# Attention projection's gate loads moved behind the next pair's weights, and the sample rows' store split over GpSimd's queue

## Chip, cores and metric

The kernel runs on one core of a Trainium2 chip. The metric is the device time of one execution in microseconds; before the change the median of three runs is 2444.72 us (2442.62 to 2445.89).

## The reference

One inference step of a hybrid decoder layer with width 2048, for a prompt of 512 tokens and 8 sequences with 4 new tokens each (544 tokens in all). An input projection feeds two branches: an mLSTM with a matrix memory, and sliding-window attention. Then the two branches are merged, projected and normalized:

```python
br_m = hn.reshape(B, T, M_WIDTH) * jax.nn.sigmoid(o_m) * jax.nn.silu(z_m)
br_a = h_a * jax.nn.silu(z_a)
y = (jax.nn.sigmoid(g_m) * jnp.einsum('btc,cd->btd', br_m, w_proj_m)
     + jax.nn.sigmoid(g_a) * jnp.einsum('btc,cd->btd', br_a, w_proj_a))
out = jnp.einsum('btc,cd->btd', y, w_out)
return _layernorm(DN_ALPHA * x + out, ln_w, ln_b).astype(x.dtype)
```

The change touches the product with `w_proj_a` and its gate `sigmoid(g_a)`, and the store of the normalized rows of the 32 sample tokens. All is float32.

## The kernel before

Each float32 operand is split into a high part and a low remainder: ScalarE casts the weights (L208, "wh"), VectorE subtracts (L209, "wl"), and TensorE adds three products (L699 with wh, L701 with wl). Activations lie transposed, 128 features by 544 tokens.

**A pair of column tiles.** For most of the projections two neighbouring tiles of 128 output columns are computed together, by a Strassen-like scheme (`paired`, L731): seven half products (steps 0 to 6) of sums of four weight blocks b11, b12, b22, b21 and sums of activation blocks that were stored earlier. `load_a` fetches b11 and b12 (L195, 512 KB each), `load_b` b22 and b21 (L668, 512 KB each). `prepare` makes the weight sums: t1 = b11 + b12 and b11 = t1 + b22 on VectorE (L679), and in a projection that has "acc" set, b12 += b22 and b21 += b11 by accumulating DMAs on GpSimd's queue (L677). `gather` collects the seven results.

**The attention projection.** Its first eight tiles and the last two are single; the six from tile 8 (PAIR_A) to 14 (TAIL_A) are three pairs, made by `pair_a` (L1774). Each pair also needs two gate tiles of 128x544 (272 KB each) from `d_sga`, the sigmoid stored in device memory; L1787 multiplies them with the pair's results, and L1788 stores the products to `d_t`. The gate tiles come from the pool `c5`, which has two buffers, so a gate load waits until the store that last used the buffer has landed. In the loop of `paired`, the call `early()` of a pair (which issues its gate loads, L1782) comes in that pair's step 2, `load_a` of the next pair in step 3 and `load_b` in step 4:

```python
if n == 3:
    load_a(work[p])
elif n == 4:
    load_b(work[p])
```

A scheduler orders the instructions of each engine by these places in the program and by priorities (weights' preparation is raised by AHEAD); SP issues the loads in its own order and, when one has to wait, all behind it wait.

**The end.** The output rows are normalized in row tiles of 128 tokens, 0 to 3 for the prompt; row 4 stands for the 32 sample tokens, held in `zs` as 128 partitions (four groups of 512 columns by 32 tokens). Row tiles 2, 3 and the samples are finished while the products for row tiles 0 and 1 run; those two come last. `moments` takes the mean and variance of a row tile, with the power -1/2 on GpSimd (L1993). `finish(4)` scales `zs`, adds the bias by an accumulating DMA of GpSimd (L2000), and stores it by one DMA of SP (L2001), in which the output is seen as 4x32x512. SP then issues the stores of row tile 0 (L2170) and of row tile 1 (L2011); ScalarE's queue issues one of each (L2170).

Of the kernel before, what the change touches and what calls it, by code (L numbers as in the profile page):

```python
# [18 lines left out]
ALU = mybir.AluOpType  # L19
# [55 lines left out]
def _build(tc, nc, i, o, es):  # L75
# [12 lines left out]
    V, A, G, PE = nc.vector, nc.scalar, nc.gpsimd, nc.tensor  # L88
# [43 lines left out]
    state = {}  # L132
# [27 lines left out]
    mh = cst.tile([128, 8], F32, name="mh")  # L160
# [27 lines left out]
    def kview(name):  # L188
        return i[name].rearrange("(kt p) c -> p kt c", p=128)
# [145 lines left out]
    for g in range(8):  # L335
        for q in range(2):
# [13 lines left out]
            else:  # L350
                hilo(pt[:], xk2[0][k // 4 - 2][:, k % 4, 0:SEQ], xk2[1][k // 4 - 2][:, k % 4, 0:SEQ])
                x_cast = state["x_cast"]
                c = (slice(None), k - 8, slice(0, SEQ - HT))
                state["x_end"] = V.tensor_tensor(out=s1r[c], in0=pt[:, HT:SEQ], in1=s1r[c], op=ALU.subtract)
        if g % 2:
# [8 lines left out]
            else:  # L364
                hilo(src, *(xk2[p][g // 2 - 2][:, :, SEQ:T] for p in range(2)))
                c = (slice(None), slice(k4.start - 8, k4.stop - 8), slice(SEQ - HT, HT))
# [295 lines left out]
    def load_a(w):  # L662
        w["b11"], w["b12"] = (load_half(w["wv"], c0, 0) for c0 in (w["cA"], w["cB"]))

    def load_b(w):
        for n, c0 in (("b22", w["cB"]), ("b21", w["cA"])):
            w[n] = raw2()
            state["load"] = nc.sync.dma_start(w[n][:], w["wv"][:, 8:16, c0:c0 + 128])  # L668

    def prepare(w, n):  # L670


        def add(out, a, b):
            if w.get("acc") and out == a and n != 2:
                loaded = state.get(("sums", 13))
                with tc.issue_after(loaded.ins) if loaded else ExitStack():
                    G.dma_start(out=w[out][:], in_=w[b][:], accum_op=ALU.add)  # L677
            else:
                V.tensor_tensor(out=w[out][:], in0=w[a][:], in1=w[b][:], op=ALU.add)  # L679
        if n == 1:  # L680
            w["t1"] = raw2()
            add("t1", "b11", "b12")
        elif n == 2:
            add("b11", "t1", "b22")
        w["hl", n] = split(w[("b11", "t1", "b11", "b21", "b12", "b22", "b21")[n]])
        if n == (1 if w.get("acc") else 3):
            add("b12", "b12", "b22")
        elif n == (3 if w.get("acc") else 4):
            add("b21", "b21", "b11")
# [42 lines left out]
    def paired(work, plain=None, rest=()):  # L732

        steps = [(w, n) for w in work for n in range(7)]
        ready = 0
        with tc.issue_after(state["load"].ins):
            load_a(work[0])
            load_b(work[0])
        for at, (w, n) in enumerate(steps):

            while ready < min(at + 3, len(steps)):
                with tc.high_priority(offset=AHEAD), tc.issue_after(plain.ins) if plain else ExitStack():
                    prepare(*steps[ready])
                ready += 1
            p = at // 7 + 1
            if p < len(work):
                if n == 3:
                    load_a(work[p])
                elif n == 4:
                    load_b(work[p])  # L750
            if n == 2 and "early" in w:
                w["early"]()
            if at == 4:
                for _ in rest:
                    pass
            half_product(w, n)
            with tc.high_priority(offset=AHEAD):
                gather(w, n)
            if n == 6:
                w["end"](w["O1"], w["O2"])  # L760
            tick()
# [907 lines left out]
    wm, wa_, wo = kview("w_proj_m"), kview("w_proj_a"), kview("w_out")  # L1669
# [104 lines left out]
    def pair_a(ct):  # L1774

        sgs = []

        def early():
            for c in (ct, ct + 1):
                sg = c5t()  # L1780
                with tc.issue_after(state["load"].ins):
                    nc.sync.dma_start(sg[:], d_sga[c])  # L1782
                sgs.append(sg)

        def end(o1, o2):
            for c, sg, o in zip((ct, ct + 1), sgs, (o1, o2)):
                V.tensor_tensor(out=sg[:], in0=o[:], in1=sg[:], op=ALU.mult)  # L1787
                nc.sync.dma_start(d_t[c], sg[:])  # L1788
        return dict(wv=wa_, x=XA, cA=ct * 128, cB=ct * 128 + 128, scale=1.0, acc=True, end=end, early=early)

    LEAD_A, PAIR_A, TAIL_A = 6, 8, 14
    marks = []
# [37 lines left out]
    XA = operands((bah_, bal_), SA)  # L1830
# [93 lines left out]
    zs = d0.tile([128, 512], F32, name="zs")[:]  # L1924
    stt = d0.tile([128, 5, 4, 6], F32, name="stt")
    mv = d0.tile([128, 5, 4], F32, name="mv")
    ys_rows = y_s.rearrange("b t d -> (b t) d")
# [51 lines left out]
    def moments(t):  # L1979
        m = mv[:, t]  # L1980
        if t < 4:
            V.bn_aggr(m[:, 0:2], stt[:, t])
            V.tensor_scalar(m[:, 1:2], m[:, 1:2], EPS, None, op0=ALU.add)
        else:
            V.bn_stats(stt[:, t, 0], zs)
            V.bn_aggr(m[:, 0:2], stt[:, t, 0:1])
            V.scalar_tensor_tensor(m[:, 1:2], m[:, 0:1], m[:, 0:1], m[:, 1:2], op0=ALU.mult, op1=ALU.add)
            pm = sm()
            PE.matmul(pm[:, 0:2], cq, m[:, 0:2], start=True, stop=True)
            V.tensor_copy(m[:, 0:2], pm[:, 0:2])  # L1990
            V.scalar_tensor_tensor(m[:, 3:4], m[:, 0:1], m[:, 0:1], m[:, 1:2], op0=ALU.mult, op1=ALU.subtract)
            V.tensor_scalar(m[:, 1:2], m[:, 3:4], -1.0, EPS, op0=ALU.mult, op1=ALU.add)
        G.tensor_tensor(out=m[:, 2:3], in0=m[:, 1:2], in1=mh[:, 0:1], op=ALU.pow)  # L1993

    def finish(t, cuts=(0, 512, 1280, D), plain=0):

        if t == 4:
            V.scalar_tensor_tensor(zs, zs, mv[:, t, 0:1], lwq, op0=ALU.subtract, op1=ALU.mult)
            A.activation(zs, zs, AF.Copy, scale=mv[:, t, 2:3])
            G.dma_start(out=zs, in_=lbq, accum_op=ALU.add)  # L2000
            nc.sync.dma_start(ys_rows.rearrange("r (q c) -> q r c", q=4), zs)  # L2001
            return
        parts = [(c0, c1, weighed(t, c0, c1)) for c0, c1 in zip(cuts, cuts[1:])]
        added(t, parts[plain:])
        for part in parts[:plain]:
            shifted(t, *part)
# [6 lines left out]
    def weighed(t, c0, c1):  # L2013
        zt = zcol(c0, c1 - c0)[:, t]
        V.scalar_tensor_tensor(zt, zt, mv[:, t, 0:1], state["ln_w"][:, c0:c1], op0=ALU.subtract, op1=ALU.mult)
        return zt
# [12 lines left out]
    def add_rows(t):  # L2029

        zt = zcol(D - G3 * 128, G3 * 128)[:, t]
        V.scalar_tensor_tensor(zt, zt, ALPHA, rows[t][:, 0:G3 * 128], op0=ALU.mult, op1=ALU.add)
        stats(t, t + 1, 3)
        moments(t)
# [76 lines left out]
    for g in range(G3):  # L2111
        ct = 16 - G3 + g
# [30 lines left out]
    for q in range(4):  # L2143
        r, cs = slice(q * 32, q * 32 + 32), slice(q * 512, q * 512 + 512)
# [50 lines left out]
    copied = [scaled(0, q, zt) for q, zt in enumerate(state["w0"])]  # L2195
    with tc.high_priority(offset=4000):
        add_rows(1)
        w1 = [weighed(1, *c) for c in QUARTERS]
        with tc.issue_after(copied[1].ins):
            factors(1)  # L2200
        biases([(1, 0, sm())])
        scaled(1, 0, w1[0])
        for q in (1, 2, 3):
            shifted(1, *QUARTERS[q], w1[q], behind=state["stored"])
# [30 lines left out]
```

## Time and profile before

| | us |
|---|---|
| median of 3 runs | 2444.72 (2442.62 to 2445.89) |
| the profiled execution's own time | 2444.07 |
| its span | 2442.3 |
| TensorE busy | 2425.5 (99%) |
| VectorE busy | 1910.9 (78%) |
| ScalarE busy | 1251.8 (51%) |
| GpSimd busy | 528.7 (22%) |

The span runs from the first to the last instruction of the profiled execution; its own time is 1.8 us longer. Busy time is the time in which an engine computed; issuing a DMA and waiting are not counted. In the rows below, "SPq" is SP's queue of DMA issues, "PE" TensorE, "DVE" VectorE, "ACT" ScalarE, "POOL" GpSimd. A timeline's row has the start, the length, the engine, the line, the operation with out<-in, and in brackets the idle time before it with what ended that. q0 is the queue of the DMAs that GpSimd issues, q1 that of SP.

### The profile page before, as it was taken

How to read it: one execution, taken by the hardware profiler on the slowest of the kernel's cores; microseconds unless marked ns; L12 is line 12 of the kernel's file. 1: busy time of each engine (PE TensorE's matmuls, PEld its weight loads, DVE VectorE, ACT ScalarE, POOL GpSimd, SP SyncE). 2: the span in 40 equal slices, each digit the busy share in tenths (PEclk: the TensorE clock that was granted, in tenths of full speed). 3: DMA queues.
4: the chain of work that ended last, by engine and by line, in shares of the span. 5: the costliest groups of instructions: out<-in, count | busy, mean ns of one | idle time of the engine just before them, and what ended most of it. 6: DMA issues, size and time to landing. Idle time of an engine off the chain costs nothing.

```text
span 2442.3 us, 49020 instructions
## 1 busy us (share of the span) xinstructions
PE 2425.5 (99%) x19394; PEld 2371.8 (97%) x19394; DVE 1910.9 (78%) x2879; ACT 1251.8 (51%) x2074; POOL 528.7 (22%) x505
## 2 busy tenths in 40 slices
PE   9999999999999999999999999999999999999998
PEld 8999999999999999999999999999999999999997
DVE  7868888888888888987877888878865676877656
ACT  6456676676666665433433444444644444444432
POOL 4114333333333430211111221120000120111111
PEclk9999999999999999999999999999999999999999
DMA  6876676667777655677687676687764598898776
GB/s 180 204 173 158 159 166 146 159 155 177 169 171 176 164 146 146 153 228 238 180 252 241 172 237 212 183 248 222 246 203 160 181 257 245 228 237 269 204 220 192
DMA packets 569601, 479.88 MB, mean 196 GB/s; under 512 B 48604, under 2 KB 464076, under 8 KB 569116
## 3 DMA queue, kind: packets, MB, share of 16 engines
q1 hardware_dynamic: 550908, 411.48, 57.1%
q0 software_dynamic: 17984, 64.50, 13.4%
q8 instruction: 152, 2.49, 0.4%
q10 hardware_dynamic: 480, 0.79, 0.1%
q14 instruction: 77, 0.63, 0.1%
HBM read 326.35 MB, written 100.77 MB: 175 GB/s over the span
## 4 chain that ended last, share of the span: by engine, by line
PE 95%; DMA 2%; DVE 1%; issue 1%; ACT 0%; POOL 0%; DVEq 0%; SPq 0%; POOLq 0%; ACTq 0%
PE bank L699 48%; PE bank L701 24%; PE bank L218 9%; PE sm L1528 2%; PE bank L1335 1%; PE sm L1567 1%; PE sm L814 1%; PE sm L1583 1%; PE sm L865 1%; PE sm L218 1%; PE sm L2047 1%; PE sm L840 1%; PE sm L1340 1%; DMA raw<-in_w_out 1%; DMA xr<-in_x_prompt 0%
## 5 line engine op out<-in xcount | busy, mean ns | idle before, releaser
L208 ACT CAST wh<-raw 128x1024 fp32r<-128x1024 f32 x641 | 671.6, 1048 | 823.2 <-PE bank L699 698.6
L209 DVE TENSOR_TENSOR wl<-raw,wh 128x1024 fp32r<-128x1024 f32 x641 | 803.6, 1254 | 194.3 <-ACT wh L208 182.2
L699 PE MATMUL bank<-xk,wh 128*128 128x272 f32 x2336 | 323.4, 289 | 0.0
L679 DVE TENSOR_TENSOR raw<-raw,raw 128x1024 f32<-128x1024 f32 x244 | 309.5, 1269 | 14.3 <-DMA raw<-in_w_proj_a 5.7
L699 PEld LDWEIGHTS bank<-xk,wh 128*128 128x128 f32 x2336 | 303.4, 188 | 1.9 <-issue 1.4
L718 POOL TENSOR_TENSOR ev<-p,ev 128x272 f32<-128x272 f32 x85 | 117.3, 1380 | 450.0 <-ACT ev L717 423.9
L699 PE MATMUL bank<-n2h,wh 128*128 128x272 f32 x656 | 170.0, 291 | 0.0
L701 PE MATMUL bank<-xk,wl 128*128 128x272 f32 x1168 | 169.8, 287 | 0.0
L699 PE MATMUL bank<-n3h,wh 128*128 128x272 f32 x656 | 169.5, 291 | 0.2 <-ACT wh L208 0.2
L699 PE MATMUL bank<-s1h,wh 128*128 128x272 f32 x656 | 169.6, 291 | 0.0
L699 PE MATMUL bank<-n2l,wh 128*128 128x272 f32 x656 | 168.0, 287 | 0.0
L699 PE MATMUL bank<-n3l,wh 128*128 128x272 f32 x656 | 167.7, 288 | 0.0
L699 PE MATMUL bank<-s1l,wh 128*128 128x272 f32 x656 | 167.4, 287 | 0.2 <-DVE s1l L258 0.2
L699 PE MATMUL bank<-s4h,wh 128*128 128x272 f32 x656 | 167.5, 289 | 0.0
L699 PE MATMUL bank<-s4l,wh 128*128 128x272 f32 x656 | 167.0, 287 | 0.0
L701 PEld LDWEIGHTS bank<-xk,wl 128*128 128x128 f32 x1168 | 155.5, 188 | 0.1
L677 POOL DMA_DIRECT2D raw<-raw x96 | 83.2, 866 | 319.4 <-DVE ev L726 220.7
L699 PE MATMUL bank<-a11h,wh 128*128 128x272 f32 x584 | 150.5, 289 | 0.0
L699 PE MATMUL bank<-a11l,wh 128*128 128x272 f32 x584 | 149.4, 288 | 0.0
L699 PEld LDWEIGHTS bank<-n3h,wh 128*128 128x128 f32 x656 | 123.4, 188 | 2.1 <-issue 1.2
L699 PEld LDWEIGHTS bank<-s1h,wh 128*128 128x128 f32 x656 | 123.2, 188 | 1.6 <-issue 1.0
L699 PEld LDWEIGHTS bank<-n2h,wh 128*128 128x128 f32 x656 | 123.4, 188 | 1.2 <-issue 1.2
(551 smaller groups left out, 5792.5 us busy)
## 6 DMA issues: line engine op xcount, KB each, us to landing
raw<-in_w_in SPq DMA_DIRECT2D x296, 512.0 KB
raw<-raw POOLq DMA_DIRECT2D x96, 512.0 KB, 5.0
C<-in_state_mlstm_C SPq DMA_DIRECT2D x32, 1024.0 KB
out<-C SPq DMA_DIRECT2D x64, 512.0 KB
raw<-in_w_proj_a SPq DMA_DIRECT2D x32, 512.0 KB
raw<-in_w_proj_m SPq DMA_DIRECT2D x32, 512.0 KB
raw<-in_w_out SPq DMA_DIRECT2D x32, 512.0 KB
d_v<-ev SPq DMA_DIRECT2D x16, 272.0 KB
```

What stands on the lines that cost most here:

```text
L208: state["cast"] = A.copy(wh[:, k:k + n], raw[:, k:k + n])
L209: state["split"] = V.tensor_tensor(out=wl[:, k:k + n], in0=raw[:, k:k + n], in1=r32(wh[:, k:k + n]), op=ALU.subtract)
L218: PE.matmul(ps[f][:, :w], a[:, kk], b(k, c, w), start=(k == 0 and n == 0), stop=(k == 15 and n == 2))
L677: G.dma_start(out=w[out][:], in_=w[b][:], accum_op=ALU.add)
L679: V.tensor_tensor(out=w[out][:], in0=w[a][:], in1=w[b][:], op=ALU.add)
L699: PE.matmul(ps, wh[:, k], x(p, k), start=(first and k == 0 and p == 0), stop=False, skip_group_check=True)
L701: state["end"] = PE.matmul(ps, wl[:, k], x(0, k), start=False, stop=(k == 7), skip_group_check=True)
L718: G.tensor_tensor(out=c22, in0=p1, in1=c11, op=ALU.subtract)
L814: PE.matmul(pp[:, c0 + w0:c0 + 256], qs[a][:, j * 128:j * 128 + 128], kx[:, k0:k0 + 256 - w0], start=(n == 0), stop=(n == 1))
L840: PE.transpose(pt[:, b * 128:b * 128 + 128], s_[:, b, 128:256], ident)
L865: PE.matmul(po[:, b * 128:b * 128 + n], VA[:, b], p_[:, 2 * b:2 * b + n // 128], start=(b == 0 and m == 0), stop=(b == 3 and m == 1), skip ...
L1528: state["cells"] = PE.matmul(pp[:, 0:258], a[:, b * 128:b * 128 + 128], b_[:, b, f], start=(b == 0 and n == 0), stop=(b == 3 and n == 2))
```

## The change

The two gate loads of each attention pair are issued in step 4, behind both loads of the next pair, and no longer in step 2 (`early_at`). The other users of `paired` keep step 2. The sample rows are stored by four DMAs of 32x512 (64 KB each) that GpSimd issues after its power for row tile 1; SP's transfer is gone. From L1790 on, lines shift by one to three.

```diff
@@ -748,7 +748,7 @@
                     load_a(work[p])
                 elif n == 4:
                     load_b(work[p])
-            if n == 2 and "early" in w:
+            if n == w.get("early_at", 2) and "early" in w:
                 w["early"]()
             if at == 4:
                 for _ in rest:
@@ -1786,7 +1786,8 @@
             for c, sg, o in zip((ct, ct + 1), sgs, (o1, o2)):
                 V.tensor_tensor(out=sg[:], in0=o[:], in1=sg[:], op=ALU.mult)
                 nc.sync.dma_start(d_t[c], sg[:])
-        return dict(wv=wa_, x=XA, cA=ct * 128, cB=ct * 128 + 128, scale=1.0, acc=True, end=end, early=early)
+        return dict(wv=wa_, x=XA, cA=ct * 128, cB=ct * 128 + 128, scale=1.0, acc=True, end=end, early=early,
+                    early_at=4)
 
     LEAD_A, PAIR_A, TAIL_A = 6, 8, 14
     marks = []
@@ -1990,7 +1991,7 @@
             V.tensor_copy(m[:, 0:2], pm[:, 0:2])
             V.scalar_tensor_tensor(m[:, 3:4], m[:, 0:1], m[:, 0:1], m[:, 1:2], op0=ALU.mult, op1=ALU.subtract)
             V.tensor_scalar(m[:, 1:2], m[:, 3:4], -1.0, EPS, op0=ALU.mult, op1=ALU.add)
-        G.tensor_tensor(out=m[:, 2:3], in0=m[:, 1:2], in1=mh[:, 0:1], op=ALU.pow)
+        state["power"] = G.tensor_tensor(out=m[:, 2:3], in0=m[:, 1:2], in1=mh[:, 0:1], op=ALU.pow)
 
     def finish(t, cuts=(0, 512, 1280, D), plain=0):
 
@@ -1998,7 +1999,6 @@
             V.scalar_tensor_tensor(zs, zs, mv[:, t, 0:1], lwq, op0=ALU.subtract, op1=ALU.mult)
             A.activation(zs, zs, AF.Copy, scale=mv[:, t, 2:3])
             G.dma_start(out=zs, in_=lbq, accum_op=ALU.add)
-            nc.sync.dma_start(ys_rows.rearrange("r (q c) -> q r c", q=4), zs)
             return
         parts = [(c0, c1, weighed(t, c0, c1)) for c0, c1 in zip(cuts, cuts[1:])]
         added(t, parts[plain:])
@@ -2195,6 +2195,9 @@
     copied = [scaled(0, q, zt) for q, zt in enumerate(state["w0"])]
     with tc.high_priority(offset=4000):
         add_rows(1)
+        with tc.issue_after(state["power"].ins):
+            for q in range(4):
+                G.dma_start(out=ys_rows[:, q * 512:q * 512 + 512], in_=zs[q * 32:q * 32 + 32])
         w1 = [weighed(1, *c) for c in QUARTERS]
         with tc.issue_after(copied[1].ins):
             factors(1)
```

On SP, between the first and the second pair, before the change (raw_3320 and raw_3321 are b22 and b21 of the first pair, raw_24470 is b12 and raw_3347, raw_3348 are b22 and b21 of the second pair, raw_24701 is b11 of the third; c_3338 and c_3339 are the first pair's gates):

```order
L668 DMA raw_3320_24339<-in_w_proj_a 128x8x128
L668 DMA raw_3321_24341<-in_w_proj_a 128x8x128
L1782 DMA c_3338_24432<-d_sga 128x544
L1463 DMA c_3416_25122<-d_brm 128x544
L1772 DMA d_t<-c_3308_24204 128x544
L668 DMA raw_3347_24503<-in_w_proj_a 128x8x128
L1782 DMA c_3339_24434<-d_sga 128x544
L1463 DMA c_3420_25144<-d_brm 128x544
L195 DMA raw_24470<-in_w_proj_a 128x8x128
L195 DMA raw_24701<-in_w_proj_a 128x8x128
L668 DMA raw_3348_24505<-in_w_proj_a 128x8x128
L1788 DMA d_t<-c_3339_24434 128x544
```

The first pair's gates stand ahead of b12 of the second pair. The same place in the changed kernel (raw_24466 is now b12, raw_24697 b11 of the third pair, raw_3345 and raw_3346 b22 and b21 of the second, c_3347 and c_3348 the gates):

```order
L668 DMA raw_3321_24341<-in_w_proj_a 128x8x128
L1463 DMA c_3416_25122<-d_brm 128x544
L1772 DMA d_t<-c_3308_24204 128x544
L668 DMA raw_3345_24499<-in_w_proj_a 128x8x128
L1463 DMA c_3420_25144<-d_brm 128x544
L195 DMA raw_24466<-in_w_proj_a 128x8x128
L195 DMA raw_24697<-in_w_proj_a 128x8x128
L668 DMA raw_3346_24501<-in_w_proj_a 128x8x128
L1782 DMA c_3347_24503<-d_sga 128x544
L1782 DMA c_3348_24505<-d_sga 128x544
L1788 DMA d_t<-c_3348_24505 128x544
```

Both gates now stand behind b12, b11 and b21. VectorE's order around the end of the first pair is the same before and after; in the changed kernel it reads (raw_3351 is t1, raw_24464 b11 of the second pair):

```order
L209 TENSOR_TENSOR wl_24533<-raw_24464,wh_24532 128x1024
L679 TENSOR_TENSOR raw_3351_24561<-raw_24464,raw_24466 128x1024
L1787 TENSOR_TENSOR c_3348_24505<-ev_24423,c_3348_24505 128x544
L679 TENSOR_TENSOR raw_24464<-raw_3351_24561,raw_3345_24499 128x1024
L728 SCALAR_TENSOR_TENSOR ev_24422<-bank_24432,p_3330_24384 128x272
L209 TENSOR_TENSOR wl_24564<-raw_3351_24561,wh_24563 128x1024
L1787 TENSOR_TENSOR c_3347_24503<-ev_24422,c_3347_24503 128x544
L209 TENSOR_TENSOR wl_24599<-raw_24464,wh_24598 128x1024
```

The multiply with the second gate tile stands between the two weight sums of the second pair. GpSimd's end:

```order
-L2000 DMA zs<-room_29415 128x512
-L1993 TENSOR_TENSOR mv<-mv,mh 128x1
-L2231 UNCONDITIONAL_BRANCH
-L2231 ISA
+L1994 TENSOR_TENSOR mv<-mv,mh 128x1 x2
+L2001 DMA zs<-room_29415 128x512
+L1994 TENSOR_TENSOR mv<-mv,mh 128x1
+L2200 DMA out<-zs 32x512 x4
+L2234 UNCONDITIONAL_BRANCH
+L2234 ISA
```

Four stores follow the last power; on SP the row of L2001 is gone, and nothing else of the end moves.

## Rows read from the trace of the kernel before

**Rows 1.** The page: span and busy time of the engines.

```profile
span 2442.3 us, 49020 instructions
...
PE 2425.5 (99%) x19394; PEld 2371.8 (97%) x19394; DVE 1910.9 (78%) x2879; ACT 1251.8 (51%) x2074; POOL 528.7 (22%) x505
```

**Rows 2.** Waits of TensorE, whole kernel: line, releaser: us, times, longest.

```profile
PE bank L699 <- ACT wh L208: 1.3, 2, 1.1
```

**Rows 3.** Chain, 1975 to 2003 us: start, length, what.

```profile
1984.26 8.28 DMA raw<-in_w_proj_a
...
1992.66 1.24 DVE raw L679
...
1995.09 3.78 PE bank L699 x28
```

**Rows 4.** Waits of SP's queue, 1971 to 1984 us.

```profile
SPq L1782 <- DMA d_t<-c: 9.0, 1, 9.0
```

**Rows 5.** Timeline of SP, 1960 to 2024 us: start, length, what.

```profile
1973.16 0.38 SPq L668 DMA_DIRECT2D raw<-in_w_proj_a  x1
1982.59 0.32 SPq L1782 DMA_DIRECT2D c<-d_sga  x1
...
1986.94 2.33 SPq L668 DMA_DIRECT2D raw<-in_w_proj_a  x1
...
2003.83 3.66 SPq L195 DMA_DIRECT2D raw<-in_w_proj_a  x2
2007.58 1.54 SPq L668 DMA_DIRECT2D raw<-in_w_proj_a  x1
```

**Rows 6.** Timeline of VectorE, 1960 to 2024 us.

```profile
1981.51 1.23 DVE L209 TENSOR_TENSOR wl<-raw,wh 128x1024 fp32r<-128x1024 f32 x1 [1.13 <-ACT wh L208]
...
1993.80 0.72 DVE L1787 TENSOR_TENSOR c<-ev,c 128x544 f32<-128x544 f32 x1
1994.43 1.22 DVE L679 TENSOR_TENSOR raw<-raw,raw 128x1024 f32<-128x1024 f32 x1
...
2014.09 0.72 DVE L1787 TENSOR_TENSOR c<-ev,c 128x544 f32<-128x544 f32 x1
...
2016.21 1.21 DVE L209 TENSOR_TENSOR wl<-raw,wh 128x1024 fp32r<-128x1024 f32 x1
```

**Rows 7.** Timeline of ScalarE, 1960 to 2024 us.

```profile
1995.77 1.05 ACT L208 CAST wh<-raw 128x1024 fp32r<-128x1024 f32 x1 [0.73 <-DVE raw L679]
```

**Rows 8.** Windows: length, busy us by engine, PEclk, DMA share, GB/s.

```profile
1993.00:1994.00 1.00, 1.00 (x9) 0.79 (x7) 1.00 (x2) 0.01 (x1) 0.00 (x0) 1.00 1.17 302
1994.00:1995.00 1.00, 0.01 (x1) 0.00 (x0) 1.00 (x2) 1.00 (x1) 0.81 (x1) 1.00 0.78 195
```

**Rows 9.** DMA queues, 1997 to 1998 us: packets, MB, share.

```profile
q0 software_dynamic: 48, 0.20, 106.5%
```

**Rows 10.** Timeline of TensorE, 2013 to 2020 us.

```profile
2018.25 1.17 PE L701 MATMUL bank<-sumh,wl 128*128 128x272 f32 x8
```

**Rows 11.** Windows of the end, columns as in rows 8.

```profile
2434.00:2439.00 5.00, 0.00 (x0) 0.00 (x0) 0.52 (x1) 0.44 (x1) 0.00 (x0) 1.00 0.99 365
2439.50:2441.00 1.50, 0.00 (x0) 0.00 (x0) 0.00 (x0) 0.00 (x0) 0.00 (x0) 0.50 0.24 90
2441.00:2442.30 1.30, 0.00 (x0) 0.00 (x0) 0.00 (x0) 0.00 (x0) 0.00 (x0) 0.50 0.00 0
```

**Rows 12.** DMA issues, 2424 to 2443 us: KB each, us to landing.

```profile
zs<-room POOLq DMA_DIRECT2D x1, 256.0 KB, 4.8
```

**Rows 13.** Timeline of GpSimd (POOL), 2422 to 2443 us.

```profile
2425.84 0.87 POOL L2000 DMA_DIRECT2D zs<-room  x1 [0.47 <-ACT room L2161]
2429.98 0.99 POOL L1993 TENSOR_TENSOR mv<-mv,mh 128x1 f32<-128x1 f32 x1 [3.28 <-DVE mv L1983]
```

**Rows 14.** Timeline of SP, 2422 to 2443 us.

```profile
2430.70 0.61 SPq L2001 DMA_DIRECT2D out<-zs  x1
...
2434.54 3.13 SPq L2011 DMA_DIRECT2D out<-zr  x3
```

## The prediction

> **What bounds the kernel now.** I read the page first. TensorE is busy for 2425.5 of the 2442.3 us of the span [rows 1], so a change can only give back what lies in TensorE's few gaps, or behind its last product. The waits of TensorE come next. Away from the first microseconds, where it waits for inputs, its largest is on L699, for a cast of weights on ScalarE: 1.3 us in two waits, the longest 1.1 [rows 2]. The chain of waits says which gap that is: between the first two pairs of the attention projection, and what ended last there was a weight load of L195 that was issued at 1984.26 and took 8.28 us; then came the sum t1 of L679, a cast, and L699 at 1995.09 [rows 3]. So at this place DMA is late, by about a microsecond, and nowhere else inside the kernel. The end is the second place: VectorE, ScalarE and TensorE are done by about 2434.5, and the rest is output stores.
>
> Why is that load late? It is b12 of the second pair. Its buffer comes free with the L209 of step 4 of the first pair, 1981.51 + 1.23 = 1982.74 [rows 6]. But SP works its queue in order, and ahead of b12 stands the second gate tile, which waited 9.0 us for a store of d_t [rows 4] and went out at 1982.59, with a d_brm load behind it [rows 5]. So b12 left 1.5 us after it could, and with two tiles of 272 KB ahead of it.
>
> A measurement of this kernel can tell about 0.2%, 4.9 us, from no change.
>
> **The move of the gate loads.** It adds and removes no instruction: three pairs, two loads each, change places on SP. The third pair has no next pair, and its loads keep their place: nothing. For the first pair, b12 is no longer behind the gate tile. The d_brm load now ahead of it waits only for a use of its buffer long past. So b12 leaves at about 1982.8 and lands at least 1.5 us earlier; the sum t1 (1992.66) and the cast follow, and the gap of 1.1 us closes, since it is shorter than that. **Gain 1.1 us** on the path, and TensorE starts step 1 of the second pair at 1995.09 - 1.1 = 1994.0.
>
> What is late next? The gate tiles are now the last in SP's queue, behind b12, b11 of the third pair, and b21. The b21 load went out at 1986.94 + 2.33 = 1989.3 [rows 5], so the gates go out after that. The bytes in the queue are the same as before, and the queue was full: DMA share 1.17 in 1993 to 1994 and 0.78 in the next microsecond, 302 and then 195 GB/s [rows 8]. It ran dry near 1994.8. A tile that is last in a queue lands when the queue runs dry: **not before 1994.8**. The latest: with t1 earlier, GpSimd issues the accumulating copy b12 += b22 earlier, and its bytes go ahead of the gates. It moves 512 KB at 0.20 MB per us, and in 1997 to 1998, while one ran, no other queue moved a packet, though a b22 load had just been issued on SP [rows 9]: 2.6 us. And the first gate tile, loaded some 30 us before its use until now, is 272 KB more at 0.30 MB per us, 0.9 us, if some engine stood idle earlier. So 1994.8 + 2.6 + 0.9 = 1998.3 at the latest.
>
> Who waits? VectorE's order is t1, then the multiply by the second gate (L1787), and only then the sum b11 = t1 + b22 of step 2 (L679), at 1993.80 and 1994.43 [rows 6]; the cast of step 2 began at 1995.77 and took 1.05 [rows 7]. From the landing G of the second gate to the weights of step 2 is thus 0.63 + 1.34 + 1.05 = 3.0 us. TensorE wants them after the 16 matmuls of step 1's first part: 28 of them took 3.78 us [rows 3], so 16 take 2.2, and the need is at 1994.0 + 2.2 = 1996.2. The stall is G + 3.0 - 1996.2, or G - 1993.2: 1.6 to 5.1 us, and at the middle (G = 1996.5) 3.3. Both ends rest on rows that are equally near, so I take the middle. Less the 1.1 gained: **+2.2 us** (0.5 to 4.0).
>
> The same move between the second and third pair. Before, no gap of TensorE stood there. The b21 load left at 2007.58 + 1.54 = 2009.1 [rows 5] and the gates now go behind it. The earliest landing is b21 and two gates, 1.08 MB at 0.30 MB per us, after that: 2012.7. The latest adds 512 KB of weights queued ahead (1.7 us) and the accumulating copy (2.6): 2017.0. From the multiply at 2014.09 to the L209 of step 1 at 2016.21 and its end is 2.12 + 1.21 = 3.3 us [rows 6]; TensorE wants that at 2018.25 [rows 10]. So a landing up to 2014.9 costs nothing, and the latest 2.1 us. All of it moves along with the first stall. I take the middle of the cost: **+1.0 us** (0 to 2.1).
>
> One cast on ScalarE and its subtraction on VectorE swap places with their neighbours before the second pair; each waits for work that was ready, and both engines have idle time there: nothing.
>
> **The sample rows' store.** Before, one SP transfer of 256 KB was issued at 2430.70, taking 0.61 us of SP, ahead of SP's six stores for row tiles 0 and 1; the issues of the last three ended at 2434.54 + 3.13 = 2437.7 [rows 14]. The stretches of the end: 365 GB/s at a share of 0.99 from 2434 to 2439, then 90 GB/s at a share of 0.24, about 4 of 16 engines, from 2439.5 to 2441, then nothing for 1.3 us [rows 11]. The slow stretch fits the store in which the transfer's outermost size is 4. It moves 0.135 MB, which at 365 GB/s takes 0.4 us and not 1.5: 1.1 us. The first stores of row tile 0 leave 0.7 us earlier, into a time in which the DMA engines were not full. **Gain 1.8 us.** The bounds: 0.3 us, if the slow stretch is another store's, and 2.8, if the stores behind it find their engines free a microsecond sooner as well.
>
> GpSimd now issues four transfers behind the power of L1993, which ended at 2430.97. One issue takes 0.87 [rows 13]: done at 2434.5. The accumulation of 256 KB before it took 4.8 us to land [rows 12], so the four land by 2439.3, 1.7 us before the last byte now. Nothing stands behind them on GpSimd. Cost: nothing, and if that cover is gone (a landing of 4.8 us becomes 6.5), each further microsecond is a microsecond.
>
> **The sum** against the profiled execution's own 2444.07 us: 2444.07 + 2.2 + 1.0 - 1.8 = 2445.5. That execution lies 0.65 us under the median of the runs shown, 2444.72, so I forecast 2446.1: no change that can be told.
>
> **The rivals.** *The gates land in time.* SP is no longer held for 9.0 us behind a gate's buffer [rows 4], so loads that stood behind it can move up into earlier time. If the engines had room there, the queue runs dry before 1993.2 and nothing stalls. Then 2444.07 - 1.1 - 1.8 = 2441.2, or 2441.8 as a median: faster than before. It decides at a landing of 1994.3, where stall and gain are equal. Against it: a share over 1 up to 1994 [rows 8].
>
> *Both accumulating copies go wholly ahead of the gates.* +4.0 + 2.1 - 1.8 gives 2449.0 as a median, and with the small gain at the end 2450.5. For it: SP's queue stood still during such a copy [rows 9].
>
> *The end gains only the issue time.* The slow stretch may be a store of row tile 1 whose engines fell behind; then the bytes are the same and only SP's 0.61 us are saved: 2445.5 + 1.2 = 2446.7, as a median 2447.3. The Trainium skill, "DMA: Bandwidth & Descriptors", section "Rules for kernel authors", holds that spreading transfers over the issuing engines gives no bandwidth, since all use the same 16 engines, and saves issue time alone. By that rule this rival is the case; a share of 0.24 [rows 11] speaks against it, since the engines were not all at work.
>
> **How the numbers follow.** Forecast (the gates stall TensorE, the end is shorter) 0.60, with its own range 2443.5 to 2448.5; gates in time 0.20; both copies ahead 0.12; issue time alone 0.08. The range 2441.2 to 2450.2 holds the forecast, the third rival and most of the other two. Faster by over 0.2% would be below 2439.8, which needs more than both gains at once: 0.06. Slower by over 0.2% is above 2449.6: 0.12, the second rival's upper part and stalls that I don't see. Within: 0.82.
>
> **What would show it.** Right: b12's issue at about 1982.8, no wait of L699 in step 1 of the second pair, but a wait of a few microseconds in step 2, for ScalarE's cast, with VectorE's L1787 released by the load of d_sga and the gates landing last; no stretch of about 90 GB/s at the end, and the span's end about 1.8 us sooner after TensorE's last matmul. Wrong: L1787 not released by a DMA; a gap of more than 5 us; GpSimd's four stores landing after all others.

## The result and the profile after

The changed kernel takes 2449.73 us in the median of 22 runs (2446.54 to 2452.64); the kernel before, on the same chip, 2445.56 us (22 runs, 2442.07 to 2449.73). The ratio is 1.0017, with a 95% interval of 1.0010 to 1.0023: 4.2 us slower, between 2.4 and 5.6. That is clear of zero, so it is a loss, though a smaller one than the 0.2% (4.9 us) that I had said a measurement can tell. The forecast was 2446.1 in a range of 2441.2 to 2450.2. The profiled execution took 2449.24 us, with a span of 2447.5, against 2444.07 and 2442.3.

The span is 5.2 us longer in these two executions. Where that comes from is read by placing the same instructions of both side by side. VectorE's L724 of the first attention pair (step 4) and L724 of a pair some 160 us later bracket the moved loads; first the kernel before, then the changed one (timeline of VectorE: start, length, engine, line):

```profile
1986.97 0.44 DVE L724 SCALAR_TENSOR_TENSOR ev<-bank,ev 128x272 f32<-128x272 f32 x1 [1.97 <-PE bank L701]
...
2143.38 0.44 DVE L724 SCALAR_TENSOR_TENSOR ev<-bank,ev 128x272 f32<-128x272 f32 x1 [1.42 <-PE bank L701]
```

```profile
1988.35 0.44 DVE L724 SCALAR_TENSOR_TENSOR ev<-bank,ev 128x272 f32<-128x272 f32 x1 [2.38 <-PE bank L701]
...
2150.62 0.44 DVE L724 SCALAR_TENSOR_TENSOR ev<-bank,ev 128x272 f32<-128x272 f32 x1 [1.42 <-PE bank L701]
```

The bracket is 156.41 us long before and 162.27 after: **5.9 us were lost between these two rows.** The first pair itself starts 1.4 us later in the changed kernel's execution; 1.3 of that is there by 100 us into the span, where nothing was changed. The last row of VectorE (L2009) is the bracket of the end, again before and after:

```profile
2432.45 2.07 DVE L2009 SCALAR_TENSOR_TENSOR zr<-zr,mv,pk 128x512 f32<-128x512 f32 x3
```

```profile
2438.93 2.07 DVE L2009 SCALAR_TENSOR_TENSOR zr<-zr,mv,pk 128x512 f32<-128x512 f32 x3
```

From its start to the end of the span it is 2442.3 - 2432.45 = 9.85 us before, 2447.5 - 2438.93 = 8.57 after: **1.3 us were gained at the end.** Between the bracket and L2009 the changed kernel makes up another 0.8 us (it is 7.24 us behind at the bracket's second row, 6.48 at L2009); what does that is not shown.

What stands inside the longer bracket is told by the waits of TensorE from 1960 to 2060 us, in the changed kernel:

```profile
PE bank L699 <- ACT wh L208: 4.4, 1, 4.4
PE bank L701 <- DVE wl L209: 0.4, 1, 0.4
```

The wait before step 1 of the second pair [rows 2, 3] is gone. A new one of 4.4 us stands in step 2. SP's timeline and VectorE's around it:

```profile
1980.30 0.32 SPq L1463 DMA_DIRECT2D c<-d_brm  x1
1983.72 5.00 SPq L195 DMA_DIRECT2D raw<-in_w_proj_a  x2
1988.82 0.54 SPq L668 DMA_DIRECT2D raw<-in_w_proj_a  x1
1989.41 4.48 SPq L1782 DMA_DIRECT2D c<-d_sga  x2
```

```profile
1992.11 1.22 DVE L679 TENSOR_TENSOR raw<-raw,raw 128x1024 f32<-128x1024 f32 x1
1999.13 0.73 DVE L1787 TENSOR_TENSOR c<-ev,c 128x544 f32<-128x544 f32 x1 [5.80 <-issue]
1999.77 1.22 DVE L679 TENSOR_TENSOR raw<-raw,raw 128x1024 f32<-128x1024 f32 x1
```

The row of L195 holds b12 and b11 of the third pair; b12 is out at 1983.72, right after its buffer is free, and t1 (L679, 1992.11) starts without a wait. The gates are issued last, from 1989.41 on. VectorE then stands idle for 5.80 us in front of the multiply by the second gate (1999.13), with the weight sum of step 2 behind it (1999.77). The profile names no releaser here ("issue"). The trace's record of semaphores does: the semaphore of each load is updated 16 times, and for the second gate tile the last of the 16 came at 1999.05, 0.08 us ahead of the multiply. In runs 4, 1 and 8 below it came at 2000.17, 2001.43 and 1999.60, and the multiply again 0.08 us behind it. The chain of waits goes on through the cast to TensorE, and windows show the granted clock (PEclk, third column from the right):

```profile
2001.10 1.05 ACT wh L208
...
2002.20 3.09 PE bank L699 x12
2005.28 1.81 PE bank L701 x8
...
2007.72 0.99 PE bank L701 x8
```

```profile
1997.00:1999.00 2.00, 0.78 (x7) 0.56 (x5) 0.00 (x0) 0.00 (x0) 0.00 (x0) 1.00 1.15 253
2000.00:2002.00 2.00, 0.00 (x0) 0.00 (x0) 2.00 (x3) 0.90 (x1) 0.00 (x0) 0.61 0.42 147
2002.00:2007.00 5.00, 4.80 (x21) 4.81 (x22) 2.25 (x3) 1.49 (x3) 0.00 (x0) 0.50 0.53 159
2007.00:2008.00 1.00, 1.00 (x9) 1.00 (x8) 0.81 (x1) 0.64 (x2) 0.39 (x1) 0.87 0.02 9
```

From the multiply's start to TensorE's start it is 2002.20 - 1999.13 = 3.07 us, the 3.0 of the forecast. But the 12 matmuls then take 3.09 us and 8 take 1.81, where 8 at the full clock take 0.99 a little later: the granted clock had fallen to 0.50, the lower of TensorE's two levels (1.2 GHz of 2.4), while the engine stood still, and it came back by about 2007. TensorE's busy time is 2427.9 us, 2.4 more than [rows 1]. So the bracket is accounted for by +4.4 (wait), +2.4 (clock), +0.4 (the wait of L701 between the second and third pair), -1.1 (the old wait): 6.1, against 5.9 measured.

The end: GpSimd's four stores are issued behind the power; the stretches of the last 1.5 us before the last byte show no slow one of the kind in [rows 11]:

```profile
2437.47 2.08 POOL L2200 DMA_DIRECT2D out<-zs  x4
```

```profile
2444.50:2445.00 0.50, 0.00 (x0) 0.00 (x0) 0.00 (x0) 0.00 (x0) 0.00 (x0) 0.50 1.05 397
2445.00:2445.50 0.50, 0.00 (x0) 0.00 (x0) 0.00 (x0) 0.00 (x0) 0.00 (x0) 0.50 0.48 180
2445.50:2446.00 0.50, 0.00 (x0) 0.00 (x0) 0.00 (x0) 0.00 (x0) 0.00 (x0) 0.50 0.08 29
```

397 GB/s, then 180, then 29: within a microsecond the rate falls to nearly nothing, and no stretch near 90 GB/s at a share of 0.24 stands there any more.

### The profile page after: what moved, and what is told of

It reads as the page before. It is cut to its first block, busy times and chain, and to the rows that moved or that the text cites. A ratio compares the mean times of both kernels' runs of the same rounds, so it can differ in the third digit from the quotient of the medians.

```text
span 2447.5 us, 49023 instructions
## 1 busy us (share of the span) xinstructions
PE 2427.9 (99%) x19394; PEld 2374.8 (97%) x19394; DVE 1910.0 (78%) x2879; ACT 1252.3 (51%) x2074; POOL 532.5 (22%) x509
## 4 chain that ended last, share of the span: by engine, by line
PE 98%; DVE 1%; issue 0%; ACT 0%; SPq 0%; DMA 0%; DVEq 0%; ACTq 0%
PE bank L699 49%; PE bank L701 24%; PE bank L218 10%; PE sm L1528 2%; PE sm L218 2%; PE bank L1335 1%; PE sm L1567 1%; PE sm L814 1%; PE sm L1583 1%; PE sm L865 1%; PE sm L2047 1%; PE sm L840 1%; PE sm L1340 1%; PE bank L421 0%; PE sm L1515 0%
## 5 line engine op out<-in xcount | busy, mean ns | idle before, releaser
L699 PE MATMUL bank<-xk,wh 128*128 128x272 f32 x2336 | 323.4, 289 | 0.0
L679 DVE TENSOR_TENSOR raw<-raw,raw 128x1024 f32<-128x1024 f32 x244 | 309.7, 1270 | 10.1 <-DMA raw<-in_w_in 2.7
L699 PEld LDWEIGHTS bank<-xk,wh 128*128 128x128 f32 x2336 | 303.4, 188 | 1.9 <-issue 1.4
L699 PE MATMUL bank<-n2h,wh 128*128 128x272 f32 x656 | 170.0, 291 | 0.0
L701 PE MATMUL bank<-xk,wl 128*128 128x272 f32 x1168 | 169.8, 287 | 0.0
L699 PE MATMUL bank<-n3h,wh 128*128 128x272 f32 x656 | 169.5, 291 | 0.2 <-ACT wh L208 0.2
L699 PE MATMUL bank<-s1h,wh 128*128 128x272 f32 x656 | 169.6, 291 | 0.0
L699 PE MATMUL bank<-n2l,wh 128*128 128x272 f32 x656 | 167.9, 287 | 0.0
L699 PE MATMUL bank<-n3l,wh 128*128 128x272 f32 x656 | 167.7, 288 | 0.0
L699 PE MATMUL bank<-s4h,wh 128*128 128x272 f32 x656 | 167.5, 289 | 0.0
L699 PE MATMUL bank<-s1l,wh 128*128 128x272 f32 x656 | 167.3, 287 | 0.0
L699 PE MATMUL bank<-s4l,wh 128*128 128x272 f32 x656 | 167.0, 287 | 0.0
L701 PEld LDWEIGHTS bank<-xk,wl 128*128 128x128 f32 x1168 | 155.6, 188 | 0.1
L677 POOL DMA_DIRECT2D raw<-raw x96 | 83.2, 867 | 314.2 <-DVE ev L726 217.7
L699 PE MATMUL bank<-a11h,wh 128*128 128x272 f32 x584 | 150.5, 289 | 0.0
L699 PE MATMUL bank<-a11l,wh 128*128 128x272 f32 x584 | 149.4, 288 | 0.0
L699 PEld LDWEIGHTS bank<-n3h,wh 128*128 128x128 f32 x656 | 123.4, 188 | 2.1 <-issue 1.2
L699 PEld LDWEIGHTS bank<-s1h,wh 128*128 128x128 f32 x656 | 123.2, 188 | 1.6 <-issue 1.0
L699 PEld LDWEIGHTS bank<-n2h,wh 128*128 128x128 f32 x656 | 123.4, 188 | 1.2 <-issue 1.2
```

Of the source, the lines that this page charges most:

```text
L699: PE.matmul(ps, wh[:, k], x(p, k), start=(first and k == 0 and p == 0), stop=False, skip_group_check=True)
L701: state["end"] = PE.matmul(ps, wl[:, k], x(0, k), start=False, stop=(k == 7), skip_group_check=True)
```

## Experiments

My theory after the result, **A**: the gates land last, VectorE's multiply waits and holds up the weight sum behind it, TensorE waits and then runs at half the clock; the end gains 1.3 us. Its rivals are named with the runs. Each run below is one kernel; ratios are against the kernel before on the same chip.

**1. Only the gate loads moved.**

```diff
-            if n == 2 and "early" in w:
+            if n == w.get("early_at", 2) and "early" in w:
...
+                    early_at=4)
```

> Only the move of the gate loads; the sample rows are stored by SP's one transfer as before. Theory A (the gates land last, VectorE's multiply holds up the weight sum of step 2 of the second pair, TensorE waits and its clock falls): the wait of L699 for the cast stays near 4.4 us, TensorE is at a granted clock of 0.50 for some 5 us after it, and without the end's gain of 1.3 us the time is 5 to 6 us over the kernel before (ratio 1.002 to 1.0025). Rival B (the loss comes from the stores of GpSimd at the end): the time is that of the kernel before, within 1 us.

2452.17 us, ratio 1.0029 (1.0019 to 1.0038), 7.1 us slower. The waits of TensorE from 1960 to 2060 us:

```profile
PE bank L699 <- ACT wh L208: 7.1, 1, 7.1
```

So the loss is the gates', and rival B falls. The wait is longer than expected, 7.1 us (the profiled execution, 2454.61 us, is the longest of the nine), and the granted clock behind it is 0.50 from 2000 to 2010 us; the end, with SP's one store, is 9.80 us by the bracket of L2009.

**2. Only the store changed** (early_at=2, the rest as in the change).

> Only the sample rows' store on GpSimd's queue; the gates are loaded in step 2 as before. Theory A: the gap of 1.1 us before step 1 of the second pair is back, no wait of 4 us anywhere inside, and the span ends about 1.3 us sooner after VectorE's last instruction: 1 to 2 us under the kernel before. Rival B: 4 us over it.

2445.14 us, ratio 1.0001 (0.9992 to 1.0009). The end is 8.80 us by the bracket of L2009, as expected, but the time shows no gain that can be told from nothing, and the profiled execution (2448.78 us, the longest of the eleven) has a wait that I had not expected, in a place where the order of loads is that of the kernel before. Its waits, and its chain:

```profile
PE bank L699 <- ACT wh L208: 4.4, 1, 4.4
```

```profile
1986.38 11.67 DMA raw<-in_w_proj_a
...
1998.17 1.24 DVE raw L679
```

b12's load took 11.67 us here, and 8.28 in the kernel before [rows 3]. So either the store reached back to this place, or the wait changes from one execution to the next.

**3. The kernel before once more.**

> The kernel before once more, for a second profile. The kernel with only the store changed has the same order of loads between the first two pairs as the kernel before, and yet a wait of 4.4 us there where the kernel before showed 1.1. Theory E (this wait changes from one execution to the next, since b12's load is issued behind a gate load that waits and then shares the DMA engines with GpSimd's copies): the wait of L699 for the cast before step 1 of the second pair is another one than 1.1 us, anywhere from 0.5 to 4.5, and the time moves with it. Rival F (the store's change itself reached back to this place): 1.1 us again, within 0.2.

2444.37 us in its one execution. Waits of TensorE, and b12's load in the chain:

```profile
PE bank L699 <- ACT wh L208: 3.0, 1, 3.0
```

```profile
1984.15 10.22 DMA raw<-in_w_proj_a
```

Theory E holds for the wait: the same kernel, 1.1 us in one execution and 3.0 in another. That the time moves with it does not show: the two executions took 2444.07 and 2444.37 us.

**4. The changed kernel once more.**

> The changed kernel once more. Theory A: a wait of 3.5 to 7.5 us in step 2 of the second pair, with a granted clock near 0.50 behind it, and no wait before step 1. Rival: a wait that is as often small as large (under 2 us), so that the profile of the changed kernel was an unlucky one.

2451.15 us in its one execution; waits of TensorE:

```profile
PE bank L699 <- ACT wh L208: 7.0, 1, 7.0
```

The long wait is no accident of one profile: 4.4, 7.0 and 7.1 us in three executions of this order of loads.

**5. The multiplies moved behind the weights of step 2.** The end of a pair is held until step 0 of the next, and its multiplies follow the last split that was prepared; loads stay as in the change.

```diff
+            if n == 0 and held:
+                held.pop()()
...
-            if n == 6:
+            if n == 6 and "early_at" in w and p < len(work):
+                held.append(lambda w=w: w["end"](w["O1"], w["O2"], state["split"]))
+            elif n == 6:
...
+                with tc.issue_after(behind.ins) if behind else ExitStack():
+                    V.tensor_tensor(out=sg[:], in0=o[:], in1=sg[:], op=ALU.mult)
```

> The changed kernel with the multiplies by the gate tiles moved on VectorE behind the second weight sum and the splits of steps 1 and 2 of the next pair; the loads stand on SP as in the changed kernel. Theory A: the gates land as late as in the changed kernel, but nothing of TensorE waits behind them: the wait of 4.4 us and the fall of the clock are gone, and so is the gap of 1.1 us, so 2 to 3 us under the kernel before. Rival C (the weights of step 2 are late by themselves, since the accumulating copy or the queue's order holds b22 or b11 up): a wait of 3 us or more in step 2 stays, and the time is that of the changed kernel within 1.5 us.

2441.64 us, ratio 0.9985 (0.9976 to 0.9994), 3.7 us faster than the kernel before. TensorE's wait of L699 for the cast in the whole kernel, and VectorE's timeline:

```profile
PE bank L699 <- ACT wh L208: 0.2, 1, 0.2
```

```profile
1992.83 2.48 DVE L679 TENSOR_TENSOR raw<-raw,raw 128x1024 f32<-128x1024 f32 x2
...
1999.50 0.72 DVE L1793 TENSOR_TENSOR c<-ev,c 128x544 f32<-128x544 f32 x1 [1.57 <-DMA c<-d_sga]
2002.67 0.73 DVE L1793 TENSOR_TENSOR c<-ev,c 128x544 f32<-128x544 f32 x1 [2.45 <-DMA c<-d_sga]
```

Now both weight sums (x2) run in one go at 1992.83, and the multiplies wait behind them, released by the loads of d_sga ("DMA c<-d_sga"), the second at 2002.67, 13.3 us after L724 of this execution. The gates are as late as before, and nothing of TensorE waits for them. Rival C falls: the weights of step 2 were in time.

**6. A third buffer for the gates** (with the store of the change, gates in step 2).

```diff
-    c5 = pool(esC, "c5", 2)
+    c5 = pool(esC, "c5", 3)
```

> The store on GpSimd's queue, the gates in step 2 as before, and three buffers for the gate tiles instead of two. Theory A says that b12 was late since a gate load waited for a buffer ahead of it on SP: with a third buffer both gates of the first pair are loaded long before, b12 is issued when its own buffer is free (about 1982.8 on the clock of the kernel before), the gap of 1.1 us shrinks to under 0.3, no gate is late for its multiply, and the time is 2 to 3 us under the kernel before. Rival D (the gap is the DMA engines' own, busy with the same bytes whatever their order): the gap stays at 0.8 us or more and the time is 1 to 2 us under the kernel before.

2443.12 us, ratio 0.9987 (0.9978 to 0.9996), 3.2 us faster. b12 left at 1983.94, when its buffer was free, and yet t1 had to wait for it:

```profile
1994.20 1.23 DVE L679 TENSOR_TENSOR raw<-raw,raw 128x1024 f32<-128x1024 f32 x1 [0.77 <-DMA raw<-in_w_proj_a]
```

TensorE waited 1.4 us, not under 0.3: the gap is rival D's, the time theory A's. The record of b12's semaphore says what is left of the gap: 15 of the 16 updates had come by 1990.92, and the last came at 1994.08 (in run 12, with three buffers too, by 1990.65 and at 1994.56). So t1 waited for the last update alone; what held that one up is not shown. The bracket of L724 is 155.8 us.

**7. The gates in step 3**, between b12 of the next pair and b11 of the one after (early_at=3, the rest as in the change).

> The changed kernel with the gate loads in step 3: on SP behind b12 of the next pair, but ahead of b11 of the third pair and of b21. Theory A: b12 still leaves when its buffer is free, no wait before step 1; the gates are issued some 3 to 5 us sooner and have 1 MB less ahead of them, so they land before their multiply's turn or under 2 us behind it: wait in step 2 under 2 us, granted clock stays at 1.00, and the time 1 to 4 us under the kernel before. Rival C (the weights of step 2 are late by themselves): the wait of 4 us or more stays.

2442.81 us, ratio 0.9991 (0.9982 to 1.0000), 2.2 us faster. The multiply by the second gate:

```profile
1994.60 0.72 DVE L1787 TENSOR_TENSOR c<-ev,c 128x544 f32<-128x544 f32 x1 [2.46 <-DMA c<-d_sga]
```

Released by the load of d_sga again, 7.50 us after L724 (1987.10) instead of 10.8 to 13.2. TensorE's longest wait here is 1.1 us. 1 MB less ahead of the gates turns the loss into a gain, though a small one: its interval reaches 1.0000.

**8. One weight sum on VectorE instead of GpSimd's accumulating copy** (the sum b12 += b22 of the three pairs, behind step 2's split; gates as in the change).

```diff
+        if "early_at" in w:
+            if n == 2:
+                V.tensor_tensor(out=w["b12"][:], in0=w["b12"][:], in1=w["b22"][:], op=ALU.add)
...
```

> The changed kernel with the sum b12 += b22 of the three attention pairs on VectorE, behind the split of step 2, in place of GpSimd's accumulating copy. It leaves the gates last in SP's queue. If the copy holds up the gates' last bytes, as forecast with 2.6 us, the gates land 1.5 to 3 us sooner and the wait in step 2 is 2 to 4.5 us instead of 4.4 to 7.1; TensorE's stall shrinks with it and the time is 1 to 3 us over the kernel before. Rival: the queue alone sets the landing; a wait of 4.4 us or more stays.

2452.22 us, ratio 1.0029 (1.0018 to 1.0040). Waits of TensorE (L702 is L699 here), and the multiply:

```profile
PE bank L702 <- ACT wh L208: 6.2, 3, 5.1
```

```profile
1999.68 0.73 DVE L1790 TENSOR_TENSOR c<-ev,c 128x544 f32<-128x544 f32 x1 [6.45 <-issue]
```

5.1 us, inside the 4.4 to 7.1 of the changed kernel, and the multiply comes 11.5 us after L724 (1988.21), with the copy 10.8 to 13.2. My expectation failed (a wait of 2 to 4.5 us, and 1 to 3 us over the kernel before; it is about 7, and why it is above the changed kernel's is not shown). But that does not free the copy: one execution stands here against a spread of 2.4 us, and the traces tell what makes the spread. The load of the second gate tile and the copy (L677) are issued within about a microsecond of each other, and either can be first; the changed kernel's first execution, then run 4:

```profile
1993.51 0.38 SPq L1782 DMA_DIRECT2D c<-d_sga  x1
1993.63 0.91 POOL L677 DMA_DIRECT2D raw<-raw  x1 [6.65 <-DVE raw L679]
```

```profile
1992.21 0.91 POOL L677 DMA_DIRECT2D raw<-raw  x1 [6.15 <-DVE raw L679]
1992.87 0.39 SPq L1782 DMA_DIRECT2D c<-d_sga  x1
```

By its semaphore, and put on the clock of the kernel before by each execution's L724, the second gate tile landed at 1997.7 and 1997.9 where its load went out first (the changed kernel, run 11), at 1998.4 without the copy (this run), and at 2000.1, 2000.1 and 2000.3 where the copy went first (runs 4, 1 and 5). So a copy that gets ahead costs the gates about 2 us; that is read from six executions, and no run sets this order by itself. The queues of run 4 from 1996 to 1998 us, while the copy runs, and SP's queue in the changed kernel's first execution from 1994 to 1997 us, ahead of the copy:

```profile
q0 software_dynamic: 75, 0.31, 76.6%
q1 hardware_dynamic: 89, 0.19, 27.5%
```

```profile
q1 hardware_dynamic: 1271, 0.98, 111.2%
```

Beside the copy SP's queue moves 0.19 MB in 2 us; ahead of it, 0.98 MB in 3 us. The queues in 1990 to 1992 us of this run show what holds SP's queue before that:

```profile
q0 software_dynamic: 190, 0.75, 94.7%
q1 hardware_dynamic: 1, 0.00, 0.1%
```

GpSimd's own loads (of d_brm, L1701 here, 544 KB each, issued at 1984.43 and 1986.13) move 190 packets, SP's queue one, while b11 and b21 stand in it; in the changed kernel's same 2 us it is 197 and none. The kernel before has these loads at the same place (0.37 MB on GpSimd's queue and 0.03 on SP's from 1990 to 1991 us), so they are not what is new in the changed kernel.

**9. Four stores on SP.** The kernel before with this edit alone:

```diff
-            nc.sync.dma_start(ys_rows.rearrange("r (q c) -> q r c", q=4), zs)
+            for q in range(4):
+                nc.sync.dma_start(ys_rows[:, q * 512:q * 512 + 512], zs[q * 32:q * 32 + 32])
```

> The kernel before with its one store of the sample rows replaced by four stores of 32x512 at the same place on SP. Theory G (the slow stretch at the end is the one transfer, whose outermost size of 4 puts it on 4 engines): from the start of VectorE's last instructions (L2009) to the span's end 8.6 to 9.1 us, as in the three kernels with four stores on GpSimd, instead of the 9.8 us of the two with one store, and no stretch near 100 GB/s of over 0.7 us. Rival H (what helps is that the store left SP's queue): 9.6 us or more, since SP issues three more transfers ahead of the others.

2442.53 us in one execution, span 2440.6. The bracket of the end:

```profile
2432.30 2.07 DVE L2010 SCALAR_TENSOR_TENSOR zr<-zr,mv,pk 128x512 f32<-128x512 f32 x3
```

2440.6 - 2432.30 = 8.30 us, shorter than with GpSimd's four (8.57 to 9.04 in seven executions), and below the 8.6 to 9.1 that I expected. Theory G holds.

**10. One store on GpSimd.**

```diff
+            G.dma_start(out=ys_rows.rearrange("r (q c) -> q r c", q=4), in_=zs)
```

> The kernel before with the one store of 4x32x512 issued by GpSimd behind the power. Theory G: the stretch near 100 GB/s stays, since the transfer still uses 4 engines, unless GpSimd issues it early enough that it ends before the others; 9.3 us or more from L2009 to the span's end. Rival H: 8.6 to 9.1 us.

2446.81 us in one execution, span 2444.8. The bracket of the end, and a window of the slow stretch:

```profile
2434.32 2.07 DVE L2009 SCALAR_TENSOR_TENSOR zr<-zr,mv,pk 128x512 f32<-128x512 f32 x3
```

```profile
2441.80:2442.30 0.50, 0.00 (x0) 0.00 (x0) 0.00 (x0) 0.00 (x0) 0.00 (x0) 0.50 0.27 102
```

2444.8 - 2434.32 = 10.48 us, longer than the 9.85 and 9.80 us with SP's one store, and the stretch near 100 GB/s at a share of 0.27 is back: 4.3 of 16 engines. Leaving SP's queue gains nothing.

**11 and 12. Versions to beat both kernels:** run 5 with four stores on SP, and the kernel before with a third buffer and four stores on SP.

> The kernel with the late multiplies (gates loaded in step 4), and the sample rows stored by four transfers on SP. If the two gains are independent, the place between the pairs gives what it gave with the late multiplies, and the end is 8.3 us from L2009's start to the span's end instead of 8.7: 3 to 5 us under the kernel before. Rival: the end's 0.4 us can't be told in the time.

> The kernel before with a third buffer for the gate tiles and the sample rows stored by four transfers on SP. Theory A: a wait of at most 1.5 us between the first two pairs, end of 8.3 us: 2.5 to 4.5 us under the kernel before, and at or up to 1 us over the one with late multiplies, which has no wait there at all.

The first: 2441.56 us, ratio 0.9981 (0.9972 to 0.9990), **4.6 us faster than the kernel before**, with an end of 8.27 us, a bracket of L724 of 155.3 us and no wait over 0.2 us between the pairs. The second: 2442.50 us, ratio 0.9987 (0.9979 to 0.9996), end 8.31, bracket 155.6, a wait of 1.2 us. The intervals of runs 5, 6, 11 and 12 overlap, so which of them is best is not told; that each beats the kernel before is.

The brackets of L724 in one place, in us, one execution each:

| order of the loads | bracket |
|---|---|
| gates in step 2, two buffers (before, run 3, runs 2, 9, 10) | 156.4, 157.6, 160.7, 155.3, 159.3 |
| gates in step 4 (changed, run 4, run 1) | 162.3, 165.1, 165.3 |
| gates in step 4, copy replaced (run 8) | 163.9 |
| gates in step 3 (run 7) | 156.1 |
| gates in step 4, late multiply (runs 5, 11) | 154.8, 155.3 |
| gates in step 2, three buffers (runs 6, 12) | 155.8, 155.6 |

The means of the first two lines are 157.9 and 164.2: the move of the gates costs 6.4 us, and the shorter end gives 1 back. That agrees with the 2.4 to 5.6 us of the paired runs.

## Why the prediction was right, and where it was off

**The number** lies in the range, 0.5 us under its upper end, and outside the forecast's own range of 2443.5 to 2448.5. There is luck in that: the range reached so far up for the second rival. That no change could be told did not hold, since the loss is clear of zero. And by a sign that I had named as wrong, a gap of more than 5 us, two of the three executions with this order of loads (runs 4 and 1, 7.0 and 7.1 us) speak against me.

**The gap that closes** was right: b12 left when its buffer was free and the wait before step 1 went. Its size was read from one execution: 1.1 us there, but 0.7 to 4.4 in the five executions with that order of loads. The row I took for the price was near the low end of what it changes between.

**The stall in step 2** was right in its mechanism (gates last, multiply between two weight sums, 3.0 us from there to TensorE), shown by runs 5 and 7, which took the multiply out of the way or the gates forward. The formula for its size was right too. On the clock of the kernel before (its L724 at 1986.97), the second gate tile landed at 1997.7 in the changed kernel's first execution and at 2000.1 in runs 4 and 1; G - 1993.2 is then 4.5, 6.9 and 6.9, and measured are 4.4, 7.0 and 7.1, where I had forecast 3.3. The step that failed is the landing: "A tile that is last in a queue lands when the queue runs dry: **not before 1994.8**". In the kernel before b21 was last in that queue. The last of the 16 updates of its semaphore came at 1996.70, 1.9 us after the 1994.8 that I had read from the bytes; 14 had come by 1995.64. From 1996.7 my own two terms give 1997.6 with the first gate's 0.9 us, and 2000.2 with the 2.6 of the accumulating copy [rows 9]: these are the landings with the second gate ahead of the copy and behind it (run 8). This is a fit after the fact, but it tells that the copy was a right reason, and that "I take the middle" put a mean between two cases of which each execution shows one or the other.

**The clock** was missing. I had only the wait itself as the price of a stall; 2.4 us of the 5.9 are matmuls at half the clock behind it. Nothing in the kernel before showed it inside the kernel, since its wait of 1.1 us left the clock at 1.00.

**The second and third pair**: 1.0 us forecast; 0.4 and 0.6 in two executions, none in a third. Right in kind, at the low end of 0 to 2.1.

**The end**: 1.8 us forecast, 1.3 in the first pair of profiles, and about 1.1 in the mean of the brackets (8.57 to 9.04 against 9.80 and 9.85). The cause was right, the one transfer on 4 engines (runs 9 and 10); the 0.7 us that I gave to SP's freed queue did not come, since with all four stores on SP the end was shorter still (8.30). The Trainium skill, "DMA: Bandwidth & Descriptors", in the section on why a DMA increments its semaphore by 16, gives this as a rule: a transfer uses the largest number of engines up to 16 that divides the outermost sizes of both its sides. The trace agrees: 4 of 16 by the share of 0.24 to 0.27, for an outermost size of 4. The rule of the same page of the Trainium skill that I weighed as a rival (section "Rules for kernel authors"), that another issuing engine brings no bandwidth, holds too: with one store on GpSimd the bracket of the end is 10.48 us, with one on SP 9.80 and 9.85. It was the shape that gained.

In the sum, +2.2 + 1.0 - 1.8 = +1.4 was forecast, and +4.2 measured: the signs of all terms held, the stall was sized at half, and the clock was left out. The second rival (copies wholly ahead, 2449.0) came out nearest in the number. Between the first two pairs it is what runs 4 and 1 show, and the first profile does not; its 2.1 us between the second and third pair did not come, and it too left out the clock.

## What to carry to other kernels

Before a load is moved behind others "since it isn't needed yet", look at the instruction that uses it and at what stands behind that one in its engine's order: here a multiply that nobody waited for stood between two weight sums that TensorE waited for. Moving the multiply behind the sums gave back what moving the load had cost, and some 3 us more (brackets of 154.8 and 155.3 against means of 164.2 and 157.9). A load can be used when the last update of its semaphore has come (here 1996.70), and not when its queue seems to run dry (1994.8). And a stall of TensorE is priced with the matmuls behind it, at the lower clock.

## What the runs showed of the hardware

After TensorE stood still for 4.4 us the granted clock was 0.50 for about 5 us, so that this wait cost half as much again. In run 2 the same wait of 4.4 us left it at 0.50 for about 3 us of work (2001 to 2004 us). Near 3 us it went either way: run 10 waited 2.8 us and showed 0.58 in the three microseconds in which it was at work again, run 3 waited 3.0 us and showed 1.00 (windows of 1997 to 2000 us, run 10 and then run 3; PEclk third from the right):

```profile
1997.00:2000.00 3.00, 3.00 (x16) 3.00 (x17) 3.00 (x5) 1.35 (x2) 0.00 (x0) 0.58 1.02 232
```

```profile
1997.00:2000.00 3.00, 3.00 (x24) 3.00 (x25) 3.00 (x5) 2.11 (x3) 0.00 (x0) 1.00 1.01 230
```

The last of a load's 16 semaphore updates can come late by itself: for b12 it came 3.2 us after the 15th in run 6 and 3.9 in run 12, and 0.04 in the changed kernel's first execution.

And GpSimd's queue, as long as it had a megabyte of its own loads to move, left SP's queue nothing: 190 packets to 1 in 2 us, with DMA at work all the time.
